# A fixed order for ScalarE and VectorE in the gate and up phases, and operands at multiples of 1024 bytes

## The chip, the core and the metric

The kernel runs on one core of one Trainium2 chip. The metric is the device time in microseconds (us) of one execution. Before the change it is 2132.48 us, the median of three runs (2130.65, 2133.27 and 2132.48 us).

## What is computed

The reference is a two-layer trunk over 256 positions of width 2048, all in float32. What matters here is the dense part:

```
h = rms_norm(x, mix_norm);  x = x + mixer(h)          # ab_in, ab_out (layer 0) or c_in, c_out (layer 1)
h = rms_norm(x, ffn_norm);  x = x + (silu(h @ w_gate) * (h @ w_up)) @ w_down
out = rms_norm(x, final_norm)
```

The hidden width of the last part is 5632, so `w_gate` and `w_up` are 2048 x 5632 each and `w_down` is 5632 x 2048, in each of the two layers. The other projections are 2048 x 6144 (ab_in), 2048 x 4096 (c_in) and twice 2048 x 2048 (ab_out, c_out).

## The kernel before

**Products of float32 precision from float32r.** Each operand is split in a high part (`hi`, a float32r copy made by ScalarE) and a low part (`lo`, the rest, a subtraction by VectorE). `three` (L413) then adds three matmuls in PSUM: high by high (L414), high by low weights (L415) and low by high weights (L416). Every matmul is 128x128 by 128x512. The weights, which change all the time, are the moving operand (`whi`, `wlo`); the activations, which are split once per phase, are the stationary one (`xh`/`xl`, `cath`/`catl`, `fh`/`fl`, `jh`/`jl`, `ush`/`usl`).

**Steps.** All projections are one list of steps. A step takes 1 MB of weights: four tiles of 128x512 in one buffer `raw` (three buffers, L164). `load(t)` issues its transfers on SyncE's queue, four steps ahead; `prep(t)` makes `whi` and `wlo` (two buffers each), two steps ahead. A buffer of `whi` or `wlo` comes free when TensorE has done the step that used it, so the parts of step t+2 are made while step t+1 runs on TensorE.

**Gate and up phases** (`run_mixed`, L474; f in the rows). They compute two matrices at once, for two halves of the rows, with products that share operands. Eleven blocks of columns are done one after another; a block has eight steps of two kinds in the order `MIX = "NNSNSNSN"`. An N step has 8 products (24 matmuls) straight from the weights. An S step has 7 products (21 matmuls); it needs sums of weight tiles, `tt` (one buffer; made by VectorE, L204 for two of the four, then L208 for one each), and their parts, and also the parts of three of the raw tiles, `ha` and `la` (one buffer each, `prep_a`, L187). A block's products are summed in seven PSUM banks. After the last S step `up_early` adds three of the banks; after the last step `up_evac` adds the other four in five instructions (L761), applies Silu on ScalarE (L779) and multiplies (L783) into `hh`, which TensorE later transposes.

**Next to them.** The last two groups of `fh` and `fl` of a phase are made while its second step runs (`x_forms`, L351): four transposes, two scalings by ScalarE into a tile `f` with one buffer, sums by VectorE (L368), and a split. When the phase ends, `jh` and `jl` for the down phase are split from the hidden tiles.

**What sets the order.** The instructions of a block of code go through a planner, which gives each engine an order from the program's order and from estimated times; with `tc.manual_schedule` the named engines keep the program's order. In the kernel before only the start of the program (L512) is in that mode. Each engine then works through its own queue in order.

**Places in SBUF.** Pools are laid one behind the other from below (`const`, `wpool`, `resid`, `small`, then the pools of the phase) and from above (`cat`, `ffn`, `us`, ...). As the tile sizes add up, `raw`, `whi` and `wlo` start 96 bytes past a multiple of 1024; the pools of the phases from below (`xh`, `fh`, `jh`, `ha`, `la`, `tt`) 864 bytes, with some tiles of `fl` at 352; the pools from above (`cath`, `catl`, `ush`, `usl`, `hh`) 992 bytes. A stationary slice is 512 bytes of a partition, a moving one 2048 bytes.

Of the kernel before, what the change touches and what calls it, by code (L numbers as in the profile page):

```python
# [9 lines left out]
F32 = mybir.dt.float32  # L10
F32R = mybir.dt.float32r
AF = mybir.ActivationFunctionType
ALU = mybir.AluOpType
# [3 lines left out]
P = 128  # L17
S = 256
M = S // P
D = 2048  # L20
NB = 512
# [10 lines left out]
GW = D // G  # L32
EPS = 1e-6
NEG = -1e30

RC = 4
RAW_BUFS = 3
W_BUFS = 2
LOAD_AHEAD = 4
PREP_AHEAD = 2  # L40
# [3 lines left out]
MIX = "NNSNSNSN"  # L44
# [5 lines left out]
A11, A12, A22, S1, S3, S2, S4 = range(S_FORMS)  # L50
# [4 lines left out]
def trunk_kernel(  # L55
# [18 lines left out]
    nc = tc.nc  # L74

    const = ctx.enter_context(tc.tile_pool(name="const", bufs=1))
    wpool = ctx.enter_context(tc.tile_pool(name="wpool", bufs=1))
    resid = ctx.enter_context(tc.tile_pool(name="resid", bufs=1))
    small = ctx.enter_context(tc.tile_pool(name="small", bufs=2))
    sides = {}  # L80

    def open_pool(name, side):
# [32 lines left out]
    steps = []  # L115
# [67 lines left out]
    def split(hi, lo, src):  # L183
        nc.scalar.copy(hi, src)  # L184
        nc.vector.tensor_tensor(out=lo, in0=src, in1=hi.bitcast(F32), op=ALU.subtract)  # L185

    def prep_a(t):  # L187

        if t >= len(steps) or steps[t].kind != "S" or t in parts_a:
            return  # L190
        load(t)
# [5 lines left out]
    def prep(t):  # L197
        if t >= len(steps) or t in parts:
            return
        load(t)  # L200
        s, r = steps[t], raws[t]
        if s.kind == "S":
            tt = mixw[0].tile([P, RC, NB], F32, tag="tt", name="tt")
            nc.vector.tensor_tensor(  # L204
                out=tt[:, 0:2, :], in0=r[:, 0:3:2, :], in1=r[:, 1::-1, :], op=ALU.subtract
            )
            for i in range(2):
                nc.vector.tensor_tensor(  # L208
                    out=tt[:, 2 + i, :], in0=r[:, 2 + i, :], in1=tt[:, 2 * i, :], op=ALU.subtract
                )  # L210
            prep_a(t)
            r = tt
        hi = wpool.tile([P, RC, NB], F32R, tag="whi", name="whi", bufs=W_BUFS)
        lo = wpool.tile([P, RC, NB], F32R, tag="wlo", name="wlo", bufs=W_BUFS)
        if s.kind == "std":
            for h in range(2):
                split(hi[:, 2 * h : 2 * h + 2, :], lo[:, 2 * h : 2 * h + 2, :],
                      r[:, 2 * h : 2 * h + 2, :])
        else:
            split(hi, lo, r)  # L220
        parts[t] = (hi, lo)
        if s.pi in operand:
            operand[s.pi].split(s.k0 // RC)

    operand = {}
# [20 lines left out]
    first = const.tile([KD, P], F32, name="first")  # L246
# [209 lines left out]
    def end_step(t, evac):  # L456
        now[0] = 2 * t + 2
        del parts[t]
        cur[0] += 1
        evac()  # L460
        load(t + LOAD_AHEAD)
        prep(t + PREP_AHEAD)
        prep_a(t + PREP_AHEAD + 1)
# [10 lines left out]
    def run_mixed(pi, lhs, early, evac):  # L474

        mixed[0] = True
        ps, seen = {}, set()
        left = {}
        while cur[0] < len(steps) and steps[cur[0]].pi == pi:
            t = cur[0]  # L480
# [9 lines left out]
            prods = PRODUCTS[s.kind]  # L490
            for j, (q, fa, group, slot) in enumerate(prods):
                if j == 4:
                    jobs_due(2 * t + 1)
                if q not in seen:
                    ps[q] = bank(BANKS[q])
                hi, lo = (parts_a if group == "a" else parts)[t]
                left[q] -= 1
                three(ps[q], lhs.hi[i][:, fa, :], lhs.lo[i][:, fa, :], hi[:, slot, :],
                      lo[:, slot, :], q not in seen, left[q] == 0)
                seen.add(q)  # L500
            parts_a.pop(t, None)
            if s.kind == "S" and "S" not in MIX[i + 1 :]:
                now[0] = 2 * t + 2
                early(s.key, ps)
            end_step(t, lambda: evac(s.key, ps) if s.last else None)
        mixed[0] = False

    cur = [0]


    order = ExitStack()
# [4 lines left out]
    st = new_norm("mix0")  # L516
# [230 lines left out]
    def ffn(pi, st, nst):  # L747
        fpool = open_pool("ffn", "right")
        hT = Hidden(fpool)
        left, right = {}, {}  # L750

        def h_transposes(j, h):
            t = hT.new(j)
            for half in range(2):
                pt = transpose_pair(h, half * 2 * P)
                nc.scalar.copy(
                    t[:, 2 * half : 2 * half + 2, :].rearrange("p a b -> p (a b)"), pt
                )
# [4 lines left out]
        def up_early(j, ps):  # L763
            g = fpool.tile([P, M, NB], F32, tag="sg", name="sg")
            h = fpool.tile([P, M, NB], F32, tag="hh", name="hh")
            nc.scalar.copy(h[:, 0, :], ps[1])
            add(g[:, 0, :], ps[6], h[:, 0, :])
            add(h[:, 1, :], ps[7], g[:, 0, :])
            left[j], right[j] = g, h

        def up_evac(j, ps):
            g, h = left.pop(j), right.pop(j)
            add(h[:, 0, :], ps[2], h[:, 0, :])
            add(g[:, 0, :], ps[5], g[:, 0, :])
            add(g[:, 1, :], ps[5], h[:, 1, :])
            add(g[:, 0, :], ps[3], g[:, 0, :])
            add(h[:, 1, :], ps[4], h[:, 1, :])
            for m in range(M):
                nc.scalar.activation(  # L779
                    g[:, m, :], g[:, m, :], AF.Silu, scale=st.r[:, m : m + 1]  # L780
                )
            for m in range(M):
                nc.vector.scalar_tensor_tensor(  # L783
                    out=h[:, m, :], in0=h[:, m, :], scalar=st.r[:, m : m + 1], in1=g[:, m, :],
                    op0=ALU.mult, op1=ALU.mult,
                )
            later(2, lambda: h_transposes(j, h))

        run_mixed(pi, st, up_early, up_evac)
# [33 lines left out]
    gate = {}  # L823
# [202 lines left out]
```

## Time and profile before

| | |
|---|---|
| time, median of 3 runs | 2132.48 us |
| the profiled execution: time, span | 2133.32 us, 2131.3 us |
| granted TensorE clock | 0.995 |
| busy: matmul, weight load | 2094.1 us (98%), 1720.9 us (81%) |
| busy: VectorE, ScalarE | 1486.9 us (70%), 1096.6 us (51%) |
| the chain that ended last | PE 85%, DVE 8%, issue 4%, DMA 1%, ACT 1% |

By the first use of each stationary operand in the trace, the stages start at about 7 us (ab_in), 300 us (ab_out), 393 us (gate and up of layer 0), 872 us (down), 1117 us (c_in), 1307 us (c_out), 1399 us (gate and up of layer 1) and 1878 us (down). PE is the matmul engine, DVE is VectorE, ACT is ScalarE, SP is SyncE. A matmul's recorded duration (about 0.39 us) overlaps the next one, so what counts is the distance from start to start.

### The profile page before, as it was taken

How to read it: one execution, taken by the hardware profiler on the slowest of the kernel's cores; microseconds unless marked ns; L12 is line 12 of the kernel's file. 1: busy time of each engine (PE TensorE's matmuls, PEld its weight loads, DVE VectorE, ACT ScalarE, POOL GpSimd, SP SyncE). 2: the span in 40 equal slices, each digit the busy share in tenths (PEclk: the TensorE clock that was granted, in tenths of full speed). 3: DMA queues.
4: the chain of work that ended last, by engine and by line, in shares of the span. 5: the costliest groups of instructions: out<-in, count | busy, mean ns of one | idle time of the engine just before them, and what ended most of it. 6: DMA issues, size and time to landing. Idle time of an engine off the chain costs nothing.

```text
span 2131.3 us, 23728 instructions
## 1 busy us (share of the span) xinstructions
PE 2094.1 (98%) x9356; PEld 1720.9 (81%) x9356; DVE 1486.9 (70%) x1421; ACT 1096.6 (51%) x1142; POOL 17.8 (1%) x37
## 2 busy tenths in 40 slices
PE   8999999999999999999999999999999999999998
PEld 6888888887888888788888878888788878878886
DVE  4545556788888888766664565578888888866675
ACT  5444445555555555555554534555554545555554
POOL 1000000000000000000000000000000000000000
PEclk9999999999999999999999999999999999999999
DMA  6555555555555555655555555555556556555553
GB/s 236 184 173 176 180 190 185 188 187 185 200 196 192 195 197 198 227 184 191 197 194 182 178 177 177 178 182 193 198 197 197 193 191 200 188 190 188 194 197 138
DMA packets 205343, 404.78 MB, mean 190 GB/s; under 512 B 9420, under 2 KB 10032, under 8 KB 204976
## 3 DMA queue, kind: packets, MB, share of 16 engines
q1 hardware_dynamic: 203296, 397.45, 56.0%
q0 software_dynamic: 1328, 4.77, 0.7%
q8 instruction: 73, 1.20, 0.2%
q10 hardware_dynamic: 608, 1.06, 0.1%
q14 instruction: 38, 0.31, 0.0%
HBM read 401.14 MB, written 2.10 MB: 189 GB/s over the span
## 4 chain that ended last, share of the span: by engine, by line
PE 85%; DVE 8%; issue 4%; DMA 1%; ACT 1%; SPq 0%; POOLq 0%; POOL 0%; DVEq 0%; ACTq 0%
PE b L415 28%; PE b L416 28%; PE b L414 27%; DVE wlo L185 5%; PE b L320 2%; DVE sg L761 1%; DVE hh L761 1%; DMA raw<-in_ab_w_in_dram 1%; DVE tt L208 1%; DVE la L185 0%; ACT whi L184 0%; PE b L356 0%; PE b L880 0%; PE b L586 0%; DMA x<-in_x_dram 0%
## 5 line engine op out<-in xcount | busy, mean ns | idle before, releaser
L185 DVE TENSOR_TENSOR wlo<-raw,whi 128x1024 fp32r<-128x1024 f32 (+1 forms) x510 | 723.4, 1450 | 270.3 <-ACT whi L184 270.1
L184 ACT CAST whi<-raw 128x1024 fp32r<-128x1024 f32 (+1 forms) x510 | 609.7, 1233 | 374.1 <-PE b L416 332.5
L415 PE MATMUL b<-wlo,fh 128*128 128x512 f32 x1144 | 447.9, 391 | 10.5 <-DVE wlo L185 10.5
L416 PE MATMUL b<-whi,fl 128*128 128x512 f32 x1144 | 445.9, 390 | 0.0
L414 PE MATMUL b<-whi,fh 128*128 128x512 f32 x1144 | 372.2, 390 | 0.0
L416 PE MATMUL b<-whi,jl 128*128 128x512 f32 x704 | 275.8, 392 | 0.8 <-DVE jl L185 0.7
L415 PE MATMUL b<-wlo,jh 128*128 128x512 f32 x704 | 275.9, 392 | 0.4 <-DVE wlo L185 0.4
L415 PEld LDWEIGHTS b<-wlo,fh 128*128 128x128 f32 x1144 | 214.9, 188 | 62.7 <-DVE wlo L185 18.9
L414 PE MATMUL b<-whi,jh 128*128 128x512 f32 x704 | 250.6, 392 | 6.1 <-ACT jh L184 6.1
L415 PE MATMUL b<-wlo,xh 128*128 128x512 f32 x640 | 253.0, 396 | 1.9 <-DVE wlo L185 1.9
L414 PEld LDWEIGHTS b<-whi,fh 128*128 128x128 f32 x1144 | 214.6, 188 | 45.6 <-ACT whi L184 0.7
L416 PE MATMUL b<-whi,xl 128*128 128x512 f32 x640 | 251.1, 393 | 0.3 <-DVE xl L345 0.3
L416 PEld LDWEIGHTS b<-whi,fl 128*128 128x128 f32 x1144 | 214.8, 188 | 44.7
L184 ACT CAST whi<-tt 128x2048 fp32r<-128x2048 f32 x66 | 126.1, 1911 | 237.1 <-DVE tt L208 229.6
L414 PE MATMUL b<-whi,xh 128*128 128x512 f32 x640 | 243.7, 399 | 3.0 <-ACT xh L341 3.0
L185 DVE TENSOR_TENSOR wlo<-tt,whi 128x2048 fp32r<-128x2048 f32 x66 | 151.3, 2292 | 127.9 <-ACT whi L184 127.9
L185 DVE TENSOR_TENSOR jl<-h,jh 128x1024 fp32r<-128x1024 f32 x88 | 107.6, 1225 | 155.1 <-ACT jh L184 155.1
L184 ACT CAST jh<-h 128x1024 fp32r<-128x1024 f32 x88 | 92.1, 1049 | 207.6 <-PE b L415 207.6
L414 PEld LDWEIGHTS b<-whi,jh 128*128 128x128 f32 x704 | 132.9, 189 | 34.3 <-ACT jh L184 6.9
L416 PEld LDWEIGHTS b<-whi,jl 128*128 128x128 f32 x704 | 133.4, 189 | 29.7 <-DVE jl L185 2.0
L415 PEld LDWEIGHTS b<-wlo,jh 128*128 128x128 f32 x704 | 133.0, 189 | 28.5 <-DVE wlo L185 0.8
L414 PEld LDWEIGHTS b<-whi,xh 128*128 128x128 f32 x640 | 121.2, 190 | 28.4 <-ACT xh L341 3.9
(146 smaller groups left out, 2069.1 us busy)
## 6 DMA issues: line engine op xcount, KB each, us to landing
raw<-in_ffn_w_gate_dram SPq DMA_DIRECT2D x176, 512.0 KB, 3.8
raw<-in_ffn_w_up_dram SPq DMA_DIRECT2D x176, 512.0 KB, 4.8
raw<-in_ffn_w_down_dram SPq DMA_DIRECT2D x88, 1024.0 KB, 5.0
raw<-in_ab_w_in_dram SPq DMA_DIRECT2D x47, 1024.0 KB, 5.1
raw<-in_c_w_in_dram SPq DMA_DIRECT2D x32, 1024.0 KB, 5.3
raw<-in_ab_w_out_dram SPq DMA_DIRECT2D x16, 1024.0 KB, 5.1
raw<-in_c_w_out_dram SPq DMA_DIRECT2D x16, 1024.0 KB, 5.0
x<-in_x_dram SPq DMA_DIRECT2D x3, 512.0 KB, 12.6
```

Of the source, the lines that this page charges most:

```text
L184: nc.scalar.copy(hi, src)
L185: nc.vector.tensor_tensor(out=lo, in0=src, in1=hi.bitcast(F32), op=ALU.subtract)
L208: nc.vector.tensor_tensor(out=tt[:, 2 + i, :], in0=r[:, 2 + i, :], in1=tt[:, 2 * i, :], op=ALU.subtract)
L320: nc.tensor.transpose(out=pt[:, j * S + m * P : j * S + (m + 1) * P], in_=src[:, m, c0 + j * P : c0 + (j + 1) * P], identity=ident,)
L414: nc.tensor.matmul(ps, lhsT=ah, rhs=bh, start=start, stop=False)
L415: nc.tensor.matmul(ps, lhsT=ah, rhs=bl, start=False, stop=False)
L416: nc.tensor.matmul(ps, lhsT=al, rhs=bh, start=False, stop=stop)
L761: nc.vector.tensor_tensor(out=out, in0=ps, in1=other, op=ALU.add)
```

## The change

The program's order becomes the order of ScalarE and VectorE through each gate and up phase, and `run_mixed` writes that order out by steps: lists `before[t]` (run inside `prep`, between the high parts and the low parts of step t+1) and `after[t]` (run behind the matmuls of step t). High and low parts are made in two halves. In S steps but the last of a block the products that need `ha` and `la` come last instead of first. `h_transposes` is due three half steps later instead of two. Three tiles that nothing uses move the pools to multiples of 1024 bytes.

```diff
+CONST_PAD = 928
+SMALL_PAD = 256
+RIGHT_PAD = 992
...
+    small.tile([P, SMALL_PAD // 4], F32, name="small_pad", bufs=1)
+    right = ctx.enter_context(tc.tile_pool(name="right", bufs=1, side="right"))
+    right.tile([P, RIGHT_PAD // 4], F32, name="right_pad")
...
+    const.tile([P, CONST_PAD // 4], F32, name="const_pad")
...
+    def prep(t, between=()):
...
-            split(hi, lo, r)
+            for h in halves:
+                nc.scalar.copy(hi[:, h, :], r[:, h, :])
+            for fn in between:
+                fn()
+            for h in halves:
+                nc.vector.tensor_tensor(
+                    out=lo[:, h, :], in0=r[:, h, :], in1=hi[:, h, :].bitcast(F32),
+                    op=ALU.subtract,
+                )
...
-        "S": ((1, A11, "a", 0), (2, A12, "a", 2), (3, S4, "a", 1), (5, S1, "b", 0),
-              (7, S3, "b", 1), (6, S2, "b", 2), (4, A22, "b", 3)),
+        "S": ((5, S1, "b", 0), (7, S3, "b", 1), (6, S2, "b", 2), (4, A22, "b", 3),
+              (1, A11, "a", 0), (2, A12, "a", 2), (3, S4, "a", 1)),
...
+        order.enter_context(
+            tc.manual_schedule(engines={mybir.EngineType.Activation, mybir.EngineType.DVE})
+        )
...
+        for t in range(lo_t, hi_t):
+            i = (t - lo_t) % n
+            if steps[t].kind != "S":
+                continue
+            early = i == MIX.index("S") and t - 3 >= lo_t
+            (after[t - 3] if early else before[t - 2]).append(lambda t=t: combine_first(t))
+            after[t - 2].append(lambda t=t: combine_rest(t))
+            after[t - 1].append(lambda t=t: prep_a(t))
+        for t in range(lo_t + n - 1, hi_t, n):
+            first, sums_a, sums_b, gate, product = ends(steps[t].key, ps)
+            after[t - n + 1 + last_s].append(first)
+            after[t].insert(0, sums_a)
+            before[t + 1][0:0] = [sums_b, gate]
+            before[t + 2].insert(0, product)
...
+            for fn in after[t]:
+                fn()
...
+            load(t + LOAD_AHEAD)
+            if t + 1 < hi_t:
+                prep(t + PREP_AHEAD, before[t + 1])
+            else:
+                order.close()
+                prep(t + PREP_AHEAD)
+                for fn in before[t + 1] + before[t + 2]:
+                    fn()
```

`first`, `sums_a`, `sums_b`, `gate` and `product` are the instructions of `up_early` and `up_evac` in five parts: a copy and two sums; the three sums of two banks; the two sums of the last two banks; the Silu; the multiplication. `combine_first` is the sum of L204, `combine_rest` the two of L208.

## Rows read from the trace of the kernel before

**Rows 1.** Waits of PE in the first gate and up phase: us in total, times, longest

```profile
PE b L415 <- DVE wlo L185: 5.2, 10, 0.6
PE b L414 <- ACT jh L184: 3.0, 1, 3.0
```

**Rows 2.** Timeline of PE at a block's start: start us, us, instruction, idle before

```profile
615.75 0.39 PE L416 MATMUL b<-ha,fl 128*128 128x512 f32 x1
616.70 0.50 PE L415 MATMUL b<-wlo,fh 128*128 128x512 f32 x1 [0.56 <-DVE wlo L185]
617.04 0.39 PE L416 MATMUL b<-whi,fl 128*128 128x512 f32 x1
```

**Rows 3.** Timeline of DVE around that block's start, and one block later

```profile
606.36 2.28 DVE L185 TENSOR_TENSOR wlo<-raw,whi 128x2048 fp32r<-128x2048 f32 x1
609.16 0.68 DVE L761 TENSOR_TENSOR sg<-b,hh 128x512 f32<-128x512 f32 x1
609.76 1.22 DVE L204 TENSOR_TENSOR tt<-raw 128x1024 f32<-128x1024 f32 x1
...
612.10 1.75 DVE L185 TENSOR_TENSOR la<-raw,ha 128x1536 fp32r<-128x1536 f32 x1
...
614.36 2.28 DVE L185 TENSOR_TENSOR wlo<-raw,whi 128x2048 fp32r<-128x2048 f32 x1
...
649.66 2.28 DVE L185 TENSOR_TENSOR wlo<-raw,whi 128x2048 fp32r<-128x2048 f32 x1
```

**Rows 4.** Busy us by engine in one block: stretch, length, then PE, PEld, DVE, ACT, POOL

```profile
606.40:649.70 43.30, 42.74 (x192) 35.06 (x192) 35.88 (x31) 22.13 (x16) 0.00 (x0) 1.00 0.59 193
```

**Rows 5.** What reads `raw` in the first gate and up phase: ns min/median/max; landing in us

```profile
L184 ACT CAST whi<-raw x58: 1039/1912/1921, 393.4 to 869.9; 128x2048 fp32r<-128x2048 f32 x54, 128x1024 fp32r<-128x1024 f32 x4
DMA to landing us min/median/max: 3.7/4.6/8.4
```

**Rows 6.** Timeline of ACT and DVE, `x_forms` in the first steps of that phase

```profile
402.06 0.83 ACT L362 ACTIVATE f<-b,vec 128x256 f32<-128x256 f32 x2
...
408.68 0.94 ACT L184 CAST fh<-f 128x896 fp32r<-128x896 f32 x1
...
411.41 1.08 DVE L185 TENSOR_TENSOR fl<-f,fh 128x896 fp32r<-128x896 f32 x1
```

**Rows 7.** Timelines of PE, ACT and DVE where that phase ends

```profile
871.93 0.52 PE L414 MATMUL b<-whi,jh 128*128 128x512 f32 x1 [3.03 <-ACT jh L184]
...
870.84 1.99 ACT L184 CAST jh<-h 128x1024 fp32r<-128x1024 f32 x2
...
869.71 0.68 DVE L761 TENSOR_TENSOR hh<-b,hh 128x512 f32<-128x512 f32 x1
870.31 2.35 DVE L185 TENSOR_TENSOR wlo<-raw,whi 128x1024 fp32r<-128x1024 f32 x2
```

**Rows 8.** Timeline of PE in ab_out and in a down phase, each with its 42nd successor

```profile
341.20 0.64 PE L414 MATMUL b<-whi,cath 128*128 128x512 f32 x2
...
350.96 0.41 PE L414 MATMUL b<-whi,cath 128*128 128x512 f32 x1
...
1970.00 0.62 PE L414 MATMUL b<-whi,jh 128*128 128x512 f32 x2
...
1979.52 0.39 PE L416 MATMUL b<-whi,jl 128*128 128x512 f32 x1
```

**Rows 9.** Matmuls by form over the span: count, busy us, mean ns, idle before

```profile
L415 PE MATMUL b<-wlo,fh 128*128 128x512 f32 x1144 | 447.9, 391 | 10.5 <-DVE wlo L185 10.5
L415 PE MATMUL b<-wlo,jh 128*128 128x512 f32 x704 | 275.9, 392 | 0.4 <-DVE wlo L185 0.4
L415 PE MATMUL b<-wlo,xh 128*128 128x512 f32 x640 | 253.0, 396 | 1.9 <-DVE wlo L185 1.9
L415 PE MATMUL b<-la,fh 128*128 128x512 f32 x198 | 78.8, 398 | 0.0
L415 PE MATMUL b<-wlo,cath 128*128 128x512 f32 x128 | 50.5, 395 | 0.0
```

More of the change, by code (lines that the diff above doesn't have):

```diff
@@ L187, in prep_a @@
     def prep_a(t):
-        if t >= len(steps) or steps[t].kind != "S" or t in parts_a:
-            return
-        load(t)
         hi = mixw[0].tile([P, 3, NB], F32R, tag="ha", name="ha")
@@ L195, in prep_a, with combine_first, combine_rest @@
         parts_a[t] = (hi, lo)
-    def prep(t):
+    def combine_first(t):
+        load(t)
+        sums[t] = tt = mixw[0].tile([P, RC, NB], F32, tag="tt", name="tt")
+        r = raws[t]
+        nc.vector.tensor_tensor(
+            out=tt[:, 0:2, :], in0=r[:, 0:3:2, :], in1=r[:, 1::-1, :], op=ALU.subtract
+        )
+    def combine_rest(t):
+        r, tt = raws[t], sums[t]
+        for i in range(2):
+            nc.vector.tensor_tensor(
+                out=tt[:, 2 + i, :], in0=r[:, 2 + i, :], in1=tt[:, 2 * i, :], op=ALU.subtract
+            )
+    def prep(t, between=()):
         if t >= len(steps) or t in parts:
@@ L200, in prep @@
         load(t)
[L201 to L212, printed above, removed]
+        s = steps[t]
+        r = sums.pop(t) if s.kind == "S" else raws[t]
         hi = wpool.tile([P, RC, NB], F32R, tag="whi", name="whi", bufs=W_BUFS)
         lo = wpool.tile([P, RC, NB], F32R, tag="wlo", name="wlo", bufs=W_BUFS)
+        halves = [slice(0, 2), slice(2, 4)]
         if s.kind == "std":
-            for h in range(2):
-                split(hi[:, 2 * h : 2 * h + 2, :], lo[:, 2 * h : 2 * h + 2, :],
-                      r[:, 2 * h : 2 * h + 2, :])
-        else:
-            split(hi, lo, r)
+            for fn in between:
+                fn()
+            for h in halves:
+                split(hi[:, h, :], lo[:, h, :], r[:, h, :])
+        else:
+            for h in halves:
+                nc.scalar.copy(hi[:, h, :], r[:, h, :])
+            for fn in between:
+                fn()
+            for h in halves:
+                nc.vector.tensor_tensor(
+                    out=lo[:, h, :], in0=r[:, h, :], in1=hi[:, h, :].bitcast(F32),
+                    op=ALU.subtract,
+                )
         parts[t] = (hi, lo)
@@ L223, in prep @@
             operand[s.pi].split(s.k0 // RC)
+    sums = {}
     operand = {}
@@ L462, in end_step @@
         prep(t + PREP_AHEAD)
-        prep_a(t + PREP_AHEAD + 1)
     BANKS = {1: 6, 6: 7, 7: 5, 2: 0, 5: 1, 3: 2, 4: 3}
     PRODUCTS = {
-        "S": ((1, A11, "a", 0), (2, A12, "a", 2), (3, S4, "a", 1), (5, S1, "b", 0),
-              (7, S3, "b", 1), (6, S2, "b", 2), (4, A22, "b", 3)),
+        "S": ((5, S1, "b", 0), (7, S3, "b", 1), (6, S2, "b", 2), (4, A22, "b", 3),
+              (1, A11, "a", 0), (2, A12, "a", 2), (3, S4, "a", 1)),
         "N": ((2, NA11, "b", 1), (2, NA12, "b", 3), (5, NA21, "b", 0), (5, NA22, "b", 2),
@@ L472, in trunk_kernel, with run_mixed @@
     }
-    def run_mixed(pi, lhs, early, evac):
+    LAST_S = tuple(sorted(PRODUCTS["S"], key=lambda q: (1, 6, 7, 2, 5, 3, 4).index(q[0])))
+    def run_mixed(pi, lhs, ends):
         mixed[0] = True
[L477 to L480, printed above, removed]
+        order = ExitStack()
+        order.enter_context(
+            tc.manual_schedule(engines={mybir.EngineType.Activation, mybir.EngineType.DVE})
+        )
+        lo_t = cur[0]
+        hi_t = lo_t
+        while hi_t < len(steps) and steps[hi_t].pi == pi:
+            hi_t += 1
+        n = len(MIX)
+        last_s = MIX.rindex("S")
+        ps, seen, left = {}, set(), {}
+        before = {t: [] for t in range(lo_t, hi_t + 3)}
+        after = {t: [] for t in range(lo_t - 1, hi_t + 3)}
+        for t in range(lo_t, hi_t):
[12 more added lines that the diff above has]
+            before[t + 2].insert(0, product)
+        for fn in before[lo_t]:
+            fn()
+        for t in range(lo_t, hi_t):
             s = steps[t]
@@ L489, in run_mixed @@
                         left[q[0]] = left.get(q[0], 0) + 1
-            prods = PRODUCTS[s.kind]
+            prods = LAST_S if i == last_s else PRODUCTS[s.kind]
             for j, (q, fa, group, slot) in enumerate(prods):
@@ L500, in run_mixed @@
                 seen.add(q)
+            now[0] = 2 * t + 2
+            for fn in after[t]:
+                fn()
             parts_a.pop(t, None)
[L502 to L505, printed above, removed]
+            del parts[t]
+            cur[0] += 1
+            load(t + LOAD_AHEAD)
[5 more added lines that the diff above has]
+                for fn in before[t + 1] + before[t + 2]:
+                    fn()
         mixed[0] = False
@@ L761, in add @@
             nc.vector.tensor_tensor(out=out, in0=ps, in1=other, op=ALU.add)
[L763 to L787, printed above, removed]
@@ L789, in ffn, with ends, first, sums_a @@
-        run_mixed(pi, st, up_early, up_evac)
+        def ends(j, ps):
+            def first():
+                g = fpool.tile([P, M, NB], F32, tag="sg", name="sg")
+                h = fpool.tile([P, M, NB], F32, tag="hh", name="hh")
+                left[j], right[j] = g, h
+                nc.scalar.copy(h[:, 0, :], ps[1])
+                add(g[:, 0, :], ps[6], h[:, 0, :])
+                add(h[:, 1, :], ps[7], g[:, 0, :])
+            def sums_a():
+                g, h = left[j], right[j]
+                add(h[:, 0, :], ps[2], h[:, 0, :])
+                add(g[:, 0, :], ps[5], g[:, 0, :])
+                add(g[:, 1, :], ps[5], h[:, 1, :])
+            def sums_b():
+                g, h = left[j], right[j]
+                add(g[:, 0, :], ps[3], g[:, 0, :])
+                add(h[:, 1, :], ps[4], h[:, 1, :])
+            def gate():
+                g = left[j]
+                for m in reversed(range(M)):
+                    nc.scalar.activation(
+                        g[:, m, :], g[:, m, :], AF.Silu, scale=st.r[:, m : m + 1]
+                    )
+            def product():
+                g, h = left.pop(j), right.pop(j)
+                for m in range(M):
+                    nc.vector.scalar_tensor_tensor(
+                        out=h[:, m, :], in0=h[:, m, :], scalar=st.r[:, m : m + 1],
+                        in1=g[:, m, :], op0=ALU.mult, op1=ALU.mult,
+                    )
+                later(3, lambda: h_transposes(j, h))
+            return first, sums_a, sums_b, gate, product
@@ L790, in ffn @@
+        run_mixed(pi, st, ends)
         close_pool("forms", "mixw")
```

## The prediction

> **What bounds the kernel now.** I read the shares of busy time first: TensorE's matmuls cover nearly the whole span, so a gain must come from gaps between matmuls or from their distance from start to start. The waits come next. In the first gate and up phase TensorE waits for VectorE's `wlo` ten times and once, where the phase ends, for `jh` [rows 1]; the second phase has the same ten. The timeline shows one such wait [rows 2]: the matmul behind the one at 615.75 starts at 616.70, 0.95 us later, and the next 0.34 us after that. The usual distance is 0.227 (42 matmuls in 9.52 us in a down phase [rows 8]), so one wait costs 0.72 + 0.11 = 0.83 us. The page's 0.56 us is less, since it counts from the modelled end of the matmul before. VectorE's timeline says why [rows 3]: between the low part of 606.36 and the one that starts at 614.36, for the block's second step, the planner put bank sums, a weight sum and `la`, and the low part ends at 616.64, just before TensorE goes on. VectorE is busy 35.88 us of a block's 43.30 [rows 4]: it has the time, and loses it to its order.
>
> **Part 1, the fixed order in the steady state.** A step takes 24 x 0.227 = 5.44 us (N) or 21 x 0.227 = 4.76 us (S). A block is 5 x 5.44 + 3 x 4.76 = 41.5 us, with about 0.9 us for eight transposes 42.4; measured from low part to low part it is 649.66 - 606.36 = 43.30 [rows 3]. The difference is the 0.83.
>
> I follow the new order by hand through the tightest place, with 0 at the end of a block's last S step (step 6). VectorE instructions follow each other 0.08 us before the recorded end (the sum at 609.16 takes 0.68, the next starts 0.60 later [rows 3]): a bank sum costs 0.60, `combine_first` 1.14, `la` 1.67, half a low part 1.13 (two take 2.35 [rows 7]); half a high part is 1.04 [rows 5], 0.95 behind another. Step 6 releases its buffers: high halves of the next block's step 0 to 2.0, low halves 1.2 to 3.4 (needed at 5.44). Three bank sums, their banks done at 2.7 at the latest, to 5.2; `combine_first` to 6.3; two more sums to 7.5, and TensorE reaches their banks no earlier than 8.1. ScalarE has the high halves of step 1 ready at 7.4 (the buffers come free at 5.44), Silu queued behind them. The low halves end at 8.7 and 9.8; step 1 starts at 10.9. Slack 1.1 us, at the very place of today's wait. The same count gives 1 us or more at the other steps: the first half is enough for a step to begin, and with `ha` and `la` used last in S steps, `la` is due 2.7 us into the step and the S step's own buffers come free 2.0 us before it ends.
>
> In order, `combine_first` at VectorE's head could wait for a transfer, with the low part and then TensorE behind it. Transfers land 4.6 us after issue in the median, 8.4 at most [rows 5]. The buffer is free when the low part of step 7 is done, 1.4 us before 0; landing at 3.2 is 2 us before the use at 5.2, and even 8.4 in every block would cost 1.8 us of lateness less 1.1 of slack, 0.7. SyncE's queue keeps its order of loads. So I let all ten waits of a phase go: 5.2 us in ten, the longest 0.6 [rows 1], are nine like the one above and one of less than half; twice 9 x 0.83 is 14.9 us, and twice 0.5 for the short one 1.0: -15.9 us. Twice as many instructions for the low parts of a block add eight times 2 x 1.13 - 2.20 = 0.5 us on VectorE, inside its slack. What is late next is the start and the end of the phase.
>
> **Part 2, the phase's start.** `x_forms` for the last two groups are now stuck at their place in program order. They share one tile `f`, so ScalarE and VectorE hand to each other in turn: 0.83, about 0.9 of sums, 0.94 and 1.08 for the first group [rows 6], 3.8 us, about 3 for the second, which has fewer sums, and some 0.8 of hand-offs: 7.6 us. In the kernel before, the planner spread them among other work (the three rows lie 10 us apart), and TensorE waited for none. Now they lie in front of `ha`, `la`, `combine_first` and the low part of step 3. By my count step 2's last products wait 1.3 us for `ha` and 0.4 for `la`. I take +1.7 a phase, +3.4. Bounds: 0 if the slack of the first steps takes it, 4.5 a phase if TensorE gets nothing from the high parts that are ready.
>
> **Part 3, the phase's end.** Today TensorE stands 3.4 us (start to start) because `jh` sits on ScalarE behind two high halves that wait for the last step [rows 7]. The change ends the fixed order before that, and the queue in front of `jh` stays. The two bank sums, now written behind the low part of 870.31 [rows 7], guard the banks that the down phase begins in. They ended at 870.4; behind two halves they would end near 873.6, later than the 871.93 at which TensorE goes on. The planner is free again there and the sums are ready first, so I take +0.5 each, +1.0 in all, between -3 each (`jh` slips forward) and +1.7 each.
>
> **Part 4, the places.** The same moving tiles run at two distances: 42 matmuls take 9.76 us against `cath` and 9.52 us against `jh` [rows 8], 0.2324 and 0.2267. The distance in ab_out keeps to its pattern (0.228 to 0.242) whatever ScalarE and VectorE do. `cath` and `ush` start at 224 modulo 256, every other operand of a float32r matmul, moving or stationary, at 96. The change puts all at 0. If the difference of places is what counts, ab_out and c_out come to 0.2267: 768 matmuls (128 x 3 in ab_out [rows 9] and as many in c_out) by 5.7 ns = -4.4 us. `ha` and `la`, 256 from `whi` modulo 512, run at the usual distance too, so equal places are no risk that the trace knows. Bounds: 0, if it is the high address and not the remainder, and for the other side the rivals below.
>
> Here the Trainium skill speaks against the change: "TensorE: Matmul & The Clock Gate", the section on what each phase of a matmul is for, says that TensorE reads the moving operand and the weights through two independent ports, so that loading the next weights takes nothing from the running matmul. By that the place of `cath` could not matter and this part would be 0. The row of ab_out disagrees (0.2324 against 0.2267 with the same moving tiles), so I keep -4.4.
>
> **The sum.** -15.9 + 3.4 + 1.0 - 4.4 = -15.9 us. From the profiled execution, 2133.3 (its span and 2.0 around it), that is 2117.4; it stood 0.8 above the median, so 2116.6, say 2116.
>
> **The rivals.**
>
> *Every matmul gets shorter.* No float32r operand lies on a multiple of 128 today (96 modulo 128 everywhere), so the trace cannot say what an aligned one does. At the granted clock (0.995, the 2.4 GHz level) 512 columns take 0.2133 us; the distance is 13.3 ns more, just one part in sixteen. If reads that straddle lines cause that, nearly all goes: 8826 matmuls (3 x (1144 + 704 + 640 + 198) + 768 [rows 9]) by up to 13.3 ns is 117 us, and with the other parts about 2004; half of it gives 2060. For it: the round fraction. Against it: two moving places, 96 and 864 modulo 1024, have the same distance. The same page's section on the gap between matmuls gives columns by the clock and about 2.5 ns more, 215.8 ns for 512; by that rule 8826 x 10.9 ns = 96 us would go. The trace's 226.7 does not agree with it at today's places; no run here shows another place.
>
> *The waits move.* The order is fixed but TensorE's own queue is still planned from estimated times, and it may be planned for lows that come later than they do; then a wait near 0.8 us a block stays at another step. What remains is -4.4 and the phase's ends: 2128 to 2133. For it: 1.1 us of slack in 10.9 is little. Against it: nothing in the new order asks VectorE for more time than it has.
>
> *Slower: equal places collide.* If the slower distance of ab_out comes from weight reads meeting the moving reads in one part of SBUF, and 0 against 0 is such a meeting, all other 8058 matmuls go to 0.2324: +46 us, less 11 from the order, 2167. It decides from 1.4 ns a matmul on (11 us by 8058). For it: the distance does depend on places. Against it: `ha`, `la` and the weights of ab_in and the down phases, all at 96, run at the lower one.
>
> **How the numbers follow.** Forecast 2116, of its own 2106 to 2125 (the bounds of parts 2 to 4 lie 3.4 and 7.0 below the sum and 5.6, 2.4 and 4.4 above it, not all at once): 0.62. Every matmul shorter: 0.09. Waits move: 0.15. Equal places collide: 0.07, and 0.07 for a wait of a fixed order that I have not seen, which costs more than it saves. The range reaches from 2088, a quarter of the first rival's gain, to 2134, the whole of the second: about 0.8 in it. With 0.2% (4.3 us) as what a measurement can tell: faster 0.62 + 0.09 + half of 0.15 = 0.78, same 0.08, slower 0.14.
>
> **What would show it.** Right: no wait for `wlo` in the blocks of the gate and up phases, blocks of 42.4 us, 42 matmuls of ab_out in 9.52 us, one or two waits of 1 to 2 us for `ha` or `la` near the third step of a phase. Wrong: a wait in every block at another step; a distance other than 0.227 in a down phase, which decides the first and third rival at once; a wait for banks where the down phase begins.

## The result, and the profile after

The changed kernel takes 2118.94 us (median of 4 runs, 2117.12 to 2121.53) against 2132.88 us (2130.65 to 2133.28, 4 runs) on the same chip: ratio 0.9938, 95% interval 0.992 to 0.9955. The forecast was 2116. The profiled execution took 2118.62 us with a span of 2116.7, granted clock 0.994; TensorE's matmuls are busy 2086.0 us (99%), VectorE 1504.7, ScalarE 1115.7.

Where the time went, by the first use of each stationary operand in the two traces (length of the stage in us):

| stage | before | after | difference |
|---|---|---|---|
| start and ab_in | 300.42 | 299.65 | -0.8 |
| ab_out; c_out | 92.82; 92.82 | 90.68; 90.68 | -4.3 |
| gate and up, layer 0; layer 1 | 478.69; 478.68 | 474.79; 474.82 | -7.8 |
| down of layer 0, c_in | 434.58 | 434.63 | 0.0 |
| down of layer 1 to the end | 253.33 | 251.41 | -1.9 |

The first and the last row of the table are hardly the change's work. At the program's start TensorE waits 5.2 us in all for its first transfers, where it waited 6.0. Where the last down phase begins, the granted clock was 0.50, the 1.2 GHz level, for 6.8 us before (first line) and for 3.4 us after (second and third line; stretch, length, PE, PEld, DVE, ACT, POOL, clock, DMA share, GB/s):

```profile
1879.20:1886.00 6.80, 6.07 (x15) 4.79 (x15) 3.13 (x4) 0.94 (x2) 0.00 (x0) 0.50 0.44 154
1865.54:1868.95 3.41, 3.06 (x8) 1.89 (x7) 3.41 (x4) 1.83 (x3) 0.00 (x0) 0.50 0.40 135
1868.95:1872.40 3.45, 3.45 (x17) 2.82 (x16) 0.89 (x2) 0.00 (x0) 0.00 (x0) 1.00 0.50 195
```

3.4 us more at half the clock come to about 1.7 of that row's 1.9 us.

The waits of PE over the whole span (us in total, times, longest us), to hold against [rows 1], which are one phase's:

```profile
PE b L440 <- ACT jh L193: 6.1, 2, 3.0
PE b L440 <- ACT ha L193: 5.4, 2, 2.7
...
PE b L441 <- DVE wlo L194: 2.3, 2, 1.9
...
PE b L442 <- DVE jl L194: 0.7, 2, 0.4
```

The ten waits for `wlo` in each gate and up phase are gone (the two left lie in c_in and near the end). `jh` waits as before. New is `ha`, once in each phase, 2.7 us.

The same block as in [rows 4], from its first bank sum to that of the next block (columns as above), then VectorE's timeline in it, which answers [rows 3], and one matmul of PE:

```profile
601.64:644.10 42.46, 42.46 (x193) 35.09 (x192) 36.64 (x38) 22.94 (x25) 0.00 (x0) 1.00 0.58 198
```

```profile
601.64 0.69 DVE L828 TENSOR_TENSOR sg<-b,hh 128x512 f32<-128x512 f32 x1 [0.75 <-ACT hh L837]
...
607.81 1.22 DVE L208 TENSOR_TENSOR tt<-raw 128x1024 f32<-128x1024 f32 x1
...
610.14 2.35 DVE L241 TENSOR_TENSOR wlo<-raw,whi 128x1024 fp32r<-128x1024 f32 x2
...
644.10 0.69 DVE L828 TENSOR_TENSOR sg<-b,hh 128x512 f32<-128x512 f32 x1 [0.75 <-ACT hh L837]
...
613.51 0.39 PE L441 MATMUL b<-wlo,fh 128*128 128x512 f32 x1
```

A block takes 42.46 us instead of 43.30, and PE is busy for all of it. VectorE, in the written order, ends the low halves of the block's second step at 612.49 (610.14 + 2.35), and the first matmul that waits for them starts at 613.51: 1.0 us later. The planner put TensorE's own queue in another order too, so the wait could have gone because TensorE asks later. It does not: counted from the phase's first, the matmul that waited before is the 987th, this one the 984th.

PE's timeline in ab_out, a matmul and its 42nd successor, answering [rows 8]: 9.52 us, where it was 9.76.

```profile
339.55 0.61 PE L440 MATMUL b<-whi,cath 128*128 128x512 f32 x2
...
349.07 0.39 PE L440 MATMUL b<-whi,cath 128*128 128x512 f32 x1
```

Now what the change costs. PE at the start of the first gate and up phase, then ScalarE and VectorE there, which answers [rows 6], and the granted clock (the third figure from the end) of two stretches:

```profile
403.51 0.60 PE L382 MATMUL b<-ident,x 128*128 128x128 f32 x4
...
404.64 0.40 PE L442 MATMUL b<-whi,fl 128*128 128x512 f32 x1
407.73 1.39 PE L440 MATMUL b<-ha,fh 128*128 128x512 f32 x3 [2.69 <-ACT ha L193]
```

```profile
398.56 0.83 ACT L388 ACTIVATE f<-b,vec 128x256 f32<-128x256 f32 x2
401.11 0.94 ACT L193 CAST fh<-f 128x896 fp32r<-128x896 f32 x1 [1.73 <-DVE f L394]
404.14 0.84 ACT L388 ACTIVATE f<-b,vec 128x256 f32<-128x256 f32 x2 [2.09 <-PE b L382]
405.47 0.83 ACT L193 CAST fh<-f 128x768 fp32r<-128x768 f32 x1 [0.49 <-DVE f L394]
406.21 1.47 ACT L193 CAST ha<-raw 128x1536 fp32r<-128x1536 f32 x1
...
402.09 1.09 DVE L194 TENSOR_TENSOR fl<-f,fh 128x896 fp32r<-128x896 f32 x1 [1.06 <-ACT fh L193]
```

```profile
407.73:411.40 3.67, 3.67 (x9) 2.78 (x10) 3.67 (x3) 2.56 (x3) 0.00 (x0) 0.54 0.21 41
411.50:415.00 3.50, 3.50 (x17) 2.90 (x16) 3.46 (x5) 1.00 (x2) 0.00 (x0) 1.00 0.92 308
```

The first group is scaled at 398.56 and copied at 401.11; the second group's transposes stand in TensorE's own queue until 403.51, and ScalarE, bound to its order, stands 2.09 us before it can scale them, with `ha` two places behind. Only the last 1.0 us of that is the transposes' doing: the tile `f` has one buffer, and VectorE reads the first group from it until 403.18 (402.09 + 1.09), while the scaling starts at 404.14. TensorE stands from 404.64 to 407.73 (3.09, 2.86 over the usual distance). Then the granted clock is 0.54 for 3.7 us, the 1.2 GHz level: eight matmuls follow each other at 0.427 instead of 0.227, another 1.6 us.

PE, ACT and DVE where the phase ends, answering [rows 7]:

```profile
861.70 0.39 PE L442 MATMUL b<-whi,fl 128*128 128x512 f32 x1
865.12 0.54 PE L440 MATMUL b<-whi,jh 128*128 128x512 f32 x1 [3.03 <-ACT jh L193]
...
862.12 1.99 ACT L193 CAST whi<-raw 128x1024 fp32r<-128x1024 f32 x2 [3.87 <-PE b L442]
864.02 1.99 ACT L193 CAST jh<-h 128x1024 fp32r<-128x1024 f32 x2
...
863.17 0.68 DVE L828 TENSOR_TENSOR hh<-b,hh 128x512 f32<-128x512 f32 x1
863.77 2.35 DVE L194 TENSOR_TENSOR wlo<-raw,whi 128x1024 fp32r<-128x1024 f32 x2
```

Nothing has moved: the same stand for `jh` behind two high halves, the same bank sums ahead of the low halves.

### The profile page after: what moved, and what is told of

It is laid out like the page before. It is cut to its first block, busy times and chain, and to the rows that moved or that the text cites. A ratio compares the mean times of both kernels' runs of the same rounds, so it can differ in the third digit from the quotient of the medians.

```text
span 2116.7 us, 24028 instructions
## 1 busy us (share of the span) xinstructions
PE 2086.0 (99%) x9356; PEld 1722.0 (81%) x9356; DVE 1504.7 (71%) x1597; ACT 1115.7 (53%) x1318; POOL 17.8 (1%) x37
## 4 chain that ended last, share of the span: by engine, by line
PE 95%; DVE 1%; DMA 1%; ACT 1%; issue 1%; SPq 0%; POOLq 0%; POOL 0%; ACTq 0%; DVEq 0%
PE b L440 31%; PE b L442 31%; PE b L441 31%; PE b L346 2%; DMA raw<-in_ab_w_in_dram 1%; DVE wlo L194 1%; ACT whi L193 0%; PE b L382 0%; PE b L961 0%; PE b L653 0%; ACT junk L929 0%; DVE vt L949 0%; DVE vt L945 0%; PE b L697 0%; ACT ha L193 0%
## 5 line engine op out<-in xcount | busy, mean ns | idle before, releaser
L194 DVE TENSOR_TENSOR wlo<-raw,whi 128x1024 fp32r<-128x1024 f32 x400 | 471.7, 1219 | 244.4 <-ACT whi L193 244.3
L193 ACT CAST whi<-raw 128x1024 fp32r<-128x1024 f32 x400 | 400.0, 1049 | 257.8 <-PE b L442 217.4
L440 PE MATMUL b<-whi,fh 128*128 128x512 f32 x1144 | 381.1, 392 | 0.0
L237 ACT CAST whi<-raw 128x1024 fp32r<-128x1024 f32 x220 | 220.3, 1050 | 177.0 <-PE b L442 93.4
L241 DVE TENSOR_TENSOR wlo<-raw,whi 128x1024 fp32r<-128x1024 f32 x220 | 258.9, 1218 | 34.3 <-ACT whi L237 34.3
L237 ACT CAST whi<-tt 128x1024 fp32r<-128x1024 f32 x132 | 134.7, 1053 | 128.7 <-PE b L442 90.3
L241 DVE TENSOR_TENSOR wlo<-tt,whi 128x1024 fp32r<-128x1024 f32 x132 | 157.2, 1220 | 58.0 <-ACT whi L237 58.0
```

The lines of the kernel that those rows point to most:

```text
L237: nc.scalar.copy(hi[:, h, :], r[:, h, :])
L241: nc.vector.tensor_tensor(out=lo[:, h, :], in0=r[:, h, :], in1=hi[:, h, :].bitcast(F32), op=ALU.subtract,)
L440: nc.tensor.matmul(ps, lhsT=ah, rhs=bh, start=start, stop=False)
```

## The experiments

Theory: the written order takes the ten waits a phase away and costs a stand at the phase's start; the places matter only as a difference between the two operands of a matmul. Rivals: halves or the new order of products do it; alignment as such does it.

**The two halves of the change alone.** `e1_places` is the kernel before with the three pads, `e2_order` the changed one without them.

```diff
+CONST_PAD = 928
+SMALL_PAD = 256
+RIGHT_PAD = 992
```

> The kernel before with the three unused tiles alone, so that raw, whi, wlo, the pools of the phases from below and those from above all start at multiples of 1024 bytes; the order is left as it was. Theory (the difference between the places of the stationary and the moving operand sets the distance of matmuls): ab_out and c_out come to 0.2267 us a matmul as in the kernel after, each 2.1 us shorter, the ten waits for wlo in each gate and up phase stay, and the time falls by 4.3 us to about 2128.5. Rival (the shorter ab_out and c_out of the kernel after come from something else in it): no change, 2132.9. A second rival (a part of the order's gain was really the places): more than 8 us.

Measured 2126.17 against 2131.95 us, ratio 0.9974 (0.9965 to 0.9984). The time fell by 5.8 us, 1.5 more than the theory's 4.3. In the trace ab_out and c_out take 90.68 us each, 4.3 us less together as expected; the gate and up phases stay at 478.76 and 478.75 with their ten waits (PE's waits in the first):

```profile
PE b L423 <- DVE wlo L192: 5.5, 10, 0.6
```

> The kernel after without the three unused tiles: the fixed order, halves and the order of products alone, operands at 96, 864 and 992 bytes as before. Theory: the two parts add up. ab_out and c_out stay at 92.8 us each (0.2324 us a matmul), no wait in a block, the wait of 2.7 us for ha at the start of each gate and up phase stays, and the time is that of the kernel after plus 4.3 us, 2123.2. Rival (the parts hang together, since the slack of the blocks was won by the places): waits come back in the blocks and the time is above 2127.

Measured 2125.52 us, ratio 0.9971 (0.9961 to 0.9982). ab_out is back at 92.82; the gate and up phases take 475.26 and 475.36, with `ha` waiting 5.4 us in two. The time is 2.3 us above the theory's 2123.2 and below the rival's 2127; in its trace the last down phase runs 6.8 us at half the clock, where the changed kernel has 3.4. The two parts add up (-5.8 and -6.4 against -13.9 in another set of runs), with no gain of one from the other to be seen beyond 2 us, and stage by stage each trace has its own part and not the other's.

**A difference of places, or a multiple?** `e4_right_128` moves only the pools from above, from 992 to 864 bytes past a multiple of 1024; nothing lies on a multiple of 128.

```diff
+RIGHT_PAD = 128
...
+    right = ctx.enter_context(tc.tile_pool(name="right", bufs=1, side="right"))
+    right.tile([P, RIGHT_PAD // 4], F32, name="right_pad")
```

> The kernel before with one unused tile of 128 bytes at the upper end alone: the pools from above start at 864 bytes past a multiple of 1024 instead of 992, everything from below stays (96 and 864). Theory (the difference of places counts, not the multiple): all operands are then 96 modulo 256 with differences of 0 or 256 modulo 512, so ab_out and c_out run at 0.2267 us a matmul and take 90.7 us instead of 92.8, though nothing lies at a multiple of 128; the time is about 2128.6. Rival (an operand must lie on a multiple of 1024, or of 128): they stay at 92.8 us and 2132.9.

Measured 2126.95 us (one run), ab_out and c_out 90.61 each: all of part 4 without any alignment.

`e8_diff` is the changed kernel with `raw`, `whi` and `wlo` left at 0; the pools of the phases from below, `ha` and `la` among them, start at 128 bytes, those from above at 64.

```diff
-SMALL_PAD = 256
-RIGHT_PAD = 992
+SMALL_PAD = 384
+RIGHT_PAD = 928
```

> The kernel after with other unused tiles: the pools of the phases from below start 128 bytes past a multiple of 1024, those from above 64 bytes past one, raw, whi and wlo stay at 0. Theory (the difference of places between the stationary and the moving operand modulo 256 sets the distance; 128 is the slower one): xh, fh and jh against whi and wlo run at 0.2324 us a matmul, 7464 matmuls by 5.7 ns, +42.6 us, 2161; ha and la against fh, both at 128, stay at 0.2267; cath and ush at 64 lie between 0.2267 and 0.2324 or at one of them. Rival (only the multiple counts): ha and la are slow too. Second rival (only a place of 224 modulo 256 or the upper addresses are slow): everything stays at 0.2267 and the time at 2119.

Measured 2167.95 us (one run), 49 above the changed kernel. PE's timeline in its last down phase, a matmul and its 42nd successor, and then a stretch of a block with both kinds (26 distances between its last two rows):

```profile
1950.15 0.40 PE L441 MATMUL b<-wlo,jh 128*128 128x512 f32 x1
...
1959.95 0.40 PE L442 MATMUL b<-whi,jl 128*128 128x512 f32 x1
```

```profile
634.19 0.39 PE L441 MATMUL b<-la,fh 128*128 128x512 f32 x1
...
635.55 0.63 PE L440 MATMUL b<-whi,fh 128*128 128x512 f32 x2
...
636.69 0.39 PE L442 MATMUL b<-whi,fl 128*128 128x512 f32 x1
...
642.73 0.40 PE L442 MATMUL b<-whi,fl 128*128 128x512 f32 x1
```

`whi` and `wlo` at 0 against `jh` at 128: 9.80 us for 42, 0.2333 each. `la` and `ha`, which lie at 128 too, against `fh` and `fl` at 128: six distances from 634.19 to 635.55, 0.2273 each, while `whi` and `wlo` against the same `fh` and `fl` take 0.2323 a little later (6.04 us by 26). ab_out, with `cath` at 64 against `whi` at 0, takes 93.10 us in place of 90.68; there 42 matmuls take 9.80 us as well (344.09 to 353.89), 0.2333 each. Alignment as such gives nothing. The time is 7 us above the theory's 2161, which had counted 0.2324 for the down phases (0.2333 here) and nothing for `cath` and `ush`.

**The stand at the phase's start.** `e3_forms_early` calls `x_forms` for the sixth group one half step earlier and leaves the seventh where it was.

```diff
-        later(2, lambda: x_transposes(st, n))
+        if st.mixed and n == 3:
+            later(1, lambda: x_forms(st, xs[n], 2 * n))
+            later(2, lambda: x_forms(st, xs[n], 2 * n + 1))
+        else:
+            later(2, lambda: x_transposes(st, n))
```

> The kernel after, with the last two groups of fh and fl issued one earlier than the other: the sixth in the middle of the phase's first step, the seventh at the start of the second, instead of both there. Theory (the 2.9 us stall for ha in each phase and the half clock behind it come from the two groups' chain through ScalarE, VectorE, TensorE's transposes and one tile, placed in front of ha): half of the chain now lies in the first step, where both engines stand idle for 2.7 us, ha comes at least 2.5 us earlier, the stall is under 0.5 us and the clock does not fall; 4 us a phase, about 2111. Rival (ha is late because VectorE and ScalarE have too much work in the first three steps, wherever it is put): the stall only moves, less than 2 us gained in all.

Missed: 2116.44 us, ratio 0.9931 (0.9918 to 0.9945), 1.4 us less per phase. PE and ACT show why:

```profile
395.68 0.60 PE L382 MATMUL b<-ident,x 128*128 128x128 f32 x4
...
396.31 0.84 ACT L388 ACTIVATE f<-b,vec 128x256 f32<-128x256 f32 x2 [2.50 <-PE b L382]
```

The program asked for the transposes in the middle of the phase's first step; the planner, which still orders TensorE, put them at its end, 0.7 us earlier in the phase than in the changed kernel, and ScalarE waits for them again. TensorE still waits for `ha`, 1.3 us (1.66 from start to start), with no stretch at the lower clock behind it but with several distances of 0.33 to 0.56 us around it, where 0.227 is usual. `e5_forms_late` goes the other way.

```diff
+            later(4, lambda: x_forms(st, xs[n], 2 * n))
+            later(8, lambda: x_forms(st, xs[n], 2 * n + 1))
```

> The kernel after, with the last two groups of fh and fl issued later: the sixth at the start of the phase's third step, the seventh at the start of the fifth, both behind ha of the first S step. Issued one earlier the sixth gave back 1.4 us of the 4.4 a phase; its transposes stood at the end of TensorE's first step all the same. Theory (what is late is whatever stands behind the chain in ScalarE's and VectorE's order; the chain itself needs about 3 us a group and the slack of steps 3 to 6 holds it): no wait for ha, no wait over 0.5 us in a phase's first block, the phase 4.0 to 4.4 us shorter than in the kernel after, about 2110.5. Rival (the chain costs its hand-offs wherever it stands): a wait of 1 to 3 us comes up at a later step of the first block and less than 2 us a phase is won.

Measured 2111.44 us, ratio 0.9906 (0.9892 to 0.9921). Both gate and up phases take 470.32, 4.5 us less than in the changed kernel. ScalarE has `ha` ahead of the chain now, and PE waits for nothing there:

```profile
398.72 1.48 ACT L193 CAST ha<-raw 128x1536 fp32r<-128x1536 f32 x1
402.06 2.01 ACT L237 CAST whi<-raw 128x1024 fp32r<-128x1024 f32 x2 [1.86 <-PE b L446]
403.96 0.84 ACT L388 ACTIVATE f<-b,vec 128x256 f32<-128x256 f32 x2
```

**The stand at the phase's end.** `e6_jh_first` splits the first hidden tiles inside the written order, ahead of the parts of the down phase's first steps, and skips a turn of the accumulator banks.

```diff
+            if t + 1 == hi_t:
+                next_parts(0)
             for fn in after[t]:
                 fn()
...
                 order.close()
+                next_parts(1)
                 prep(t + PREP_AHEAD)
...
+        def next_parts(n):
+            if n == 0:
+                close_pool("forms", "mixw")
+                xpool[0] = open_pool("x_next", "left")
+                hT.split_pool = open_pool("split", "left")
+                turn["acc"] += 1
+            hT.split(n)
```

> The kernel after, with the end of a gate and up phase changed: the first part of jh and jl is made inside the fixed order, ahead of the last bank sums and of the high halves that wait for TensorE, the second part ahead of those halves too, and the down phase begins in the two banks that are summed first. Theory (3.4 us of standing and the half clock behind it come from jh standing behind two high halves on ScalarE, then from the banks): TensorE goes on about 1 us after the last step, when the second bank is free, the clock does not fall, 3 to 4 us a phase end, about 2112. Rival (jh waits for its memory or its hidden tile, not for its place in ScalarE's order): jh starts as late as before and nothing is won, 2118.9.

Measured 2113.13 us, ratio 0.9915 (0.99 to 0.9929). In the first layer the phase takes 471.61 us, 3.2 less than in the changed kernel, and TensorE goes on without a gap; in the second it takes 475.66, 0.8 more: `jh` is no longer waited for, but a bank is, 3.9 us. `e7_both` has both moves:

> Both of the above together: the groups later and jh first. Theory: the phase's start and end are 450 us apart and add up, about 2104 (8.4 us from the starts and 6 to 8 from the ends off 2118.9). Rival (either fails alone): what the two single kernels show, added.

Measured 2104.87 us, ratio 0.9876 (0.9859 to 0.9892). The first layer's phase takes 467.18, the second's 471.24, and there PE and DVE show that wait again:

```profile
1849.37 0.47 PE L444 MATMUL b<-whi,jh 128*128 128x512 f32 x1 [3.94 <-DVE sg L835]
...
1845.08 0.68 DVE L835 TENSOR_TENSOR sg<-b,sg 128x512 f32<-128x512 f32 x1
1845.68 0.68 DVE L835 TENSOR_TENSOR sg<-b,hh 128x512 f32<-128x512 f32 x1
```

The turn of the banks is odd in one layer and even in the other, so skipping one is right only once. `e11_bank`:

```diff
-                turn["acc"] += 1
+                turn["acc"] |= 1
```

> The version with both moves, and in it the skip of one turn of the accumulator banks made only where the turn is even, so that the down phase begins in the banks that are read first in both layers. Theory: in the version with both moves the second layer's gate and up phase is 4.06 us longer than the first's (471.24 against 467.18) only because its down phase begins in banks that VectorE still reads (its one wait of 3.9 us for sg L835); with the right bank both phases take about 467.2 and the wait is gone: 2104.9 - 4.1 = about 2100.8. Rival: the stand at the second phase's end has another cause as well (jh or jl late there), then a wait for jh takes the place of the one for sg and the time stays at 2103 to 2105.

Measured 2098.3 us (2097.36 to 2098.92, 4 runs) against 2132.23, ratio 0.984 (0.9826 to 0.9855): the best version, ahead of both kernels. The phases take 467.17 and 467.19, and where the second ends PE goes on without a gap:

```profile
1845.59 0.39 PE L446 MATMUL b<-whi,fl 128*128 128x512 f32 x1
1845.86 0.47 PE L444 MATMUL b<-whi,jh 128*128 128x512 f32 x1
```

That is 2.5 us below the theory. The phase accounts for 4.1 us as said; besides, the granted clock stays at 1.00 behind the phase's end, where in `e7_both` it was 0.50 for 3.4 us.

**What in the order does it?** `e9_whole` keeps the order but makes the parts in one piece; `e10_a_first` puts the products with `ha` and `la` first again, but for a block's last S step, which keeps its own new order; `e12_order_only` does both. The low parts are put in one piece like the high ones.

```diff
-            for h in halves:
-                nc.scalar.copy(hi[:, h, :], r[:, h, :])
+            nc.scalar.copy(hi, r)
...
-        "S": ((5, S1, "b", 0), (7, S3, "b", 1), (6, S2, "b", 2), (4, A22, "b", 3),
-              (1, A11, "a", 0), (2, A12, "a", 2), (3, S4, "a", 1)),
+        "S": ((1, A11, "a", 0), (2, A12, "a", 2), (3, S4, "a", 1), (5, S1, "b", 0),
+              (7, S3, "b", 1), (6, S2, "b", 2), (4, A22, "b", 3)),
```

> The changed kernel with high and low parts of gate and up steps made in one piece as before, the fixed order kept. In the changed kernel's trace the low halves of a block's step 1 end at 611.35 and 612.49, and the first matmul that uses them starts at 612.15: a low part in one piece would start at 610.14 too and end at 612.42. Theory (the halves are a needed part of what takes the waits away, the slack is smaller than the 1.1 us of my count): a wait of about 0.3 us in each block, with the first matmuls behind it slower 0.4, in 20 blocks +8: about 2127, and waits for wlo about 20 in number. Rival (my count's 1.1 us of slack): no wait comes back, 2119.

> The changed kernel with the products of S steps in the order of the kernel before (those with ha and la first), all else kept. In the changed kernel la of a block's second S step ends at 630.49, while the step starts at 629.23 and la's first use would come at 630.13; and the step's own buffers would come free 2.0 us later, so that the last S step's la, which ends at 639.5 with the step starting at 639.4, comes about 0.6 us later. Theory (the order of products is needed): about 1 us a block, 22 blocks, +15 to +25: 2134 to 2144, with waits for la or ha or wlo in every block. Rival (the order of products does nothing, VectorE and ScalarE have slack): 2119, within 0.2%.

> The changed kernel with both undone at once: high and low parts in one piece, and the products of S steps with ha and la first; what stays is the written order of ScalarE and VectorE and the places. Either alone left the time at 2118 to 2119. Theory (the written order alone takes the ten waits a phase away, as TensorE's own queue is planned and puts the products whose parts come late behind others): no wait for wlo in the blocks, 2118 to 2120. Rival (each of the two covered for the other): waits of 0.3 us and more come back in the blocks, 2124 or above.

Measured 2119.03, 2118.05 and 2118.62 us, ratios 0.994 (0.9923 to 0.9956), 0.9934 (0.9919 to 0.9949) and 0.994 (0.9923 to 0.9957): no difference from the changed kernel in any, and in the first two not what my theory said. For `e9_whole` I had taken the matmul at 612.15 for the first user of the new low part; it belongs to the step before. DVE and PE of `e9_whole`:

```profile
610.26 2.28 DVE L239 TENSOR_TENSOR wlo<-raw,whi 128x2048 fp32r<-128x2048 f32 x1
...
613.53 0.39 PE L436 MATMUL b<-wlo,fh 128*128 128x512 f32 x1
```

The first matmul that waits for it starts at 613.53, 1.0 us after its end. For `e10_a_first`, PE of that kernel and DVE:

```profile
630.54 0.84 PE L440 MATMUL b<-ha,fh 128*128 128x512 f32 x3
...
632.58 0.39 PE L441 MATMUL b<-la,fh 128*128 128x512 f32 x1
...
628.23 1.76 DVE L194 TENSOR_TENSOR la<-raw,ha 128x1536 fp32r<-128x1536 f32 x1
```

The first use of `la` lies 4.35 us behind its start. In the changed kernel the two stand at 628.73 and 633.08, 4.35 us as well. The program's order of products reaches TensorE through the planner, and here nothing of the edit got through: by the tiles that they read, all 9356 matmuls of the two traces come in the same order, and so do those of `e9_whole` and `e12_order_only`. So `e10_a_first` does not test what another order of products would do. In the first phase of `e12_order_only` PE waits for nothing but these:

```profile
PE b L435 <- ACT jh L193: 3.0, 1, 3.0
PE b L435 <- ACT ha L193: 1.9, 1, 1.9
PE b L435 <- ACT whi L236: 0.8, 1, 0.8
```

So the waits for `wlo` stay away without the halves, which add nothing that these runs can measure, and writing the products of S steps in another order changes nothing, since it does not reach TensorE. What is left is the fixed order of ScalarE and VectorE, with what belongs to it (the bank sums in parts, `h_transposes` half a step later, the order of the last S step); these smaller pieces were not taken out one by one.

## Why the prediction was right, and where its sum was not

*The order in the steady state (-15.9).* Right. `e5_forms_late`, which has no stand at the start and the old one at the end, gives the term by itself: 470.32 against 478.69 in one phase and 478.68 in the other, -16.7 us in two. My hand count left 1.1 us at the tightest place; the trace has 1.0. The mechanism is the one that I gave: VectorE's low part comes earlier, at an all but unchanged place of TensorE's queue. That `la` is due 2.7 us into a step because the program says so was wrong: TensorE's queue decides it, as `e10_a_first` shows.

*The phase's start (+3.4).* This is the step that failed in size. In place of 1.7 us a phase it cost 4.5 (`e5_forms_late` takes it away: 474.79 - 470.32 and 474.82 - 470.32), the upper bound that I had named for another reason. The path was right: the chain of `x_forms` stands in front of `ha`, and TensorE waits for `ha`. Two things were left out of the 1.7. The larger is the clock: the stand is followed by eight matmuls at the 1.2 GHz level, 1.6 us. The other is that I had the chain run through in 7.6 us with its transposes ready, though I said myself, for a rival, that TensorE's queue stays planned; the second group was scaled 1.0 us after the tile `f` was free, since its transposes stood in that queue, and the stand came to 2.9 us.

*The phase's end (+1.0).* About 0: TensorE stands 3.42 us from start to start as before, down of layer 0 is 0.15 us longer, and the bank sums kept their place. The wait for banks that I feared is real, but hidden behind `jh`: with `jh` out of the way it appeared in one layer of `e6_jh_first` and `e7_both`, 3.9 us.

*The places (-4.4).* Right: -4.3 in the stages, and `e4_right_128` with `e8_diff` show the reason given. Here the Trainium skill's rule of two independent read ports ("TensorE: Matmul & The Clock Gate", the section on what each phase of a matmul is for), by which the term would be 0, does not agree with these runs: in `e8_diff` the same stationary tiles run at 0.2273 and at 0.2323 in one block, by the place of the moving one.

The sum came within 3 us because errors met: -0.8 and -0.9 in the parts that were better than said, +5.6 at the start of the phases, and -1.9 in the last down phase with -0.8 at the program's start, which no part of the prediction had. These last 2.7 us are luck. The stage from the last down phase to the end goes with the stretch at half the clock and not with the order: it is 253.33 in the kernel before, 253.13 in `e1_places` and 253.40 in `e2_order`, each with 6.8 us of it, and 251.03 in `e4_right_128` (old order), 251.41 in the changed kernel and 251.25 in `e12_order_only`, each with 3.4; `e3_forms_early`, `e5_forms_late` and `e6_jh_first` lie between, at 252.1 to 252.2. Why one trace has more of it than another is not shown.

*The rivals.* Every matmul shorter: fell, a down phase keeps 0.227 with all operands on multiples of 1024. Waits move: they did not, no block has a wait in the trace but a phase's first, for `ha`. Slower, equal places collide: fell for equal places. That its price is near that of unequal ones (2167 said, 2167.95 in `e8_diff`) is partly chance, since other matmuls are the slow ones there, and by other amounts.

## What to carry to other kernels

An engine that is put in a written order waits in line for every engine that is still planned: for each instruction in the list, look where its producer stands in the producer's own queue. When a stand is removed, the next one behind it may already be there (banks behind `jh`), so remove, look, and remove again: that took 13.9 us to 33.9. Before an experiment is read, see whether its edit reached the engine's queue; the planner can undo it. And hold the places of both operands of a matmul against each other before aligning either.

## What the runs showed of the hardware that was not expected

- With float32r operands of these shapes the distance from matmul to matmul depends on the difference of the two operands' places in a partition: 0.2267 to 0.2273 us where it is 0 modulo 256 bytes (moving and stationary at 96 and 864, 864 and 864, 0 and 0, 128 and 128), 0.2323 to 0.2333 where it is 64 or 128. Other differences were not run, and why is not shown.
- After each stand of 3.1 to 3.4 us (from start to start) the granted clock fell to the 1.2 GHz level (0.54 over the next 3.7 us at the phase's start); after the two of `e3_forms_early`, 1.7 us, it did not. A stand of 2.3 us in c_in is the same in most runs, and the clock fell behind it in the kernel before and in the changed one but not in `e5_forms_late` and `e11_bank`. So part of a stand's price comes behind it, 1.6 us on 2.9 at the phase's start, and it differs from trace to trace.
